# A two-layer attention/S5 backbone on one core: the last two SSM blocks' spans placed behind the second block's states, the end of the down product laid out anew, and its norms without ScalarE's roots

## Chip, core and metric

One core of a Trainium2 chip runs the whole program. The metric is the device time of one execution in microseconds (us). The kernel before takes 1716.74 us (median of 3 runs, 1716.3 to 1719.77).

## What is computed

Two layers over 512 latent tokens and 256 context tokens of width 1024. Layer 0 mixes tokens by attention, layer 1 by a bidirectional S5 state-space layer; each is followed by a gated ConvFFN, and every sub-layer stands between two RMS norms with a shift, a scale and a gate. Cut to what the change touches (layer 0's ConvFFN, then layer 1's mixer):

```
h  = modulate(rms_norm(x, g_pre_ffn), shift, scale)
a  = conv3(h @ w_up) + conv_b                       # 2 x 2816 columns
x  = x + gate * rms_norm((silu(a_gate) * a_val) @ w_down, g_post_ffn)
h  = modulate(rms_norm(x, g_pre_mix), shift, scale) # input of the S5 layer
for d in (forward, reverse):                        # 64 groups of 16 channels, 64 complex states each
    hc = scan(lambda, B @ h_context)                # the context's final state is the latents' first
    hl = scan(lambda, B @ h_latent, start=hc_final)
    y += Re(C @ hl)
g  = gelu(y + d_skip * h)
o  = (g @ w_glu_a) * sigmoid(g @ w_glu_b)
```

All of it is float32.

## The kernel before

A float32 product runs as three TensorE (PE) matmuls over operands split into a high and a low part (`mm3`, L145 to L147). A weight tile of 128x1024 is loaded by SyncE (SP) into a `wraw` slot, its high part is written by ScalarE (ACT, L108) and its low part by VectorE (DVE, L109), or by GpSimd (POOL) where the plan calls the weight "pool". The result is a `whl` tile. The loads, the splits and the products are pipelined over a few slots each.

`run()` goes through the stages qkv, attention, wo (the attention's output product), ffn0 (layer 0's ConvFFN), ssm, glu and ffn1. The text speaks of these places:

- **ffn0, up product** (about 490 to 845 us). PE multiplies w_up; between the products it prepares the tables of the S5 layer. These tables (`QT`, `Ks`) are written to DRAM (`Qd`) by SP, two DMAs for each QT and four for each Ks, in the same queue as the weight loads.
- **ffn0, down product, two passes** (`ffn_down`, `dn` tiles). The first pass takes three token tiles, the second the last three latent ones (tiles 3, 4, 5). The activation's split `hs` (ACT L927, DVE L928) rotates over `nhs` slots. The last four weights of a pass (`ends=4`) are held, so that one tile can be finished after the other. In the second pass the context half of the S5 scan (`ssm_contexts`) runs beside the product; it reads matrices `Pt` (SP, L1391).
- **end of a pass** (`done`, `begin`, `end`). For each finished tile: gate and sum of squares (ACT L726, DVE L727), a root (`rsqrt`), the residual (DVE L732, then a store to `x2`), the next norm's sum of squares and root, the scale (POOL L1022) and the shift (DVE L1023). The result `po` goes through a DMA into `xc`. The gate, shift and scale rows are loaded by `rows_of` (L996).
- **rsqrt** (L157 to L170). With `self.bits` it is eight small DVE instructions (a bit trick and three Newton steps), without it five on DVE and a square root on ACT, which needs another activation table.
- **ssm**. `ssm_turn` copies `xc` to `xq` (L1405) and turns it on PE (`pu`, L1410). `ssm_inputs` multiplies by the `Pt` matrices (`pi`, L1435) into B. `ssm_spans` (L1460 to L1464) scans spans of eight positions in seven steps on DVE: spans[0] and spans[1] serve blocks 0 and 1 (256 elements a partition each), spans[2] blocks 2 and 3 together (512). `local(i)` carries over the span ends in seven serial steps of four small instructions (L1473 to L1476) for blocks 2i and 2i+1. `states(blk)` adds the carries to all positions (L1591, L1595, L1602), `outputs(blk)` multiplies by the `Qd` matrices on PE (`py`, L1620), `turned(blk)` turns the result (`pg`, L1640), splits it into `gT` (DVE L1646) and multiplies by a GLU weight.

The order of each engine's instructions is set when the program is built: a scheduler with a model of times places them, engine by engine. `tc.issue_after(x)` gives the instructions traced inside it an order behind x, but only those on x's own engine. `W.behind` uses it for weight splits. In `ssm` the loop over the blocks reads:

```
first(0); local(0)
for blk in range(4):
    if blk == 2:
        first(1); local(1)
    turned(blk, outputs(blk, states(blk)))
```

`first(1)` runs spans[2] to its end. Nothing before the change holds it behind `states`.

Of the kernel before, what the change touches and what calls it, by code (L numbers as in the profile page):

```python
# [9 lines left out]
FT = mybir.dt.float32  # L10
# [3 lines left out]
AF = mybir.ActivationFunctionType  # L14
OP = mybir.AluOpType
# [4 lines left out]
P = 128  # L20
# [111 lines left out]
class Kernel:  # L132
# [619 lines left out]
    def wo(self):  # L752
        tc, nc = self.tc, self.nc
        self.ps = ps = tc.alloc_tile_pool(name="psC", bufs=1, space=PSUM, reuse_waits="tile")
        self.kv.release()
        self.bits = False
        self.actc = self.pool("actB1", "right")
        self.actp = self.pool("actB0", "right")
        late = self.pool("late", "right")
        wk = self.pool("wkC", "right")  # L760
        self.xd = self.dram.tile([TOK, D], FT, name="xd0")
        self.act = [[p.tile([P, 2, n], FR, name=f"b{n}_{kk}") for kk in range(KD)]
                    for p, n in ((self.actp, LAT), (self.actc, CTX))]
        acts = ((self.act[0], CTX, TOK, 0), (self.act[1], 0, CTX, 0))
        gates = [self.row(wk, 0, 1, 0, lc, f"gate{lc}", 1) for lc in range(2)]
        xn = {}

        def each(t, acc):
            x = self.post(t, acc, gates, self.x_rows, wk, 2)
            nc.sync.dma_start(self.xd[t * P:(t + 1) * P, :], x)  # L770
            xn[t] = self.renorm(x, late)
            if t % 2 and t > NTC:
                turn(t - 1, range(KD // 2))

        def turn(t, kps):
            self.transpose_norm(ps, late, [xn[t], xn[t + 1]], self.cols[0, 1], int(t < NTC), acts, t * P, kps)

        def turn_last():

            for kp in range(KD // 2):  # L780
                turn(0, (kp,))
                yield
            late.release()

        self.turn_last = turn_last()
        for i, tiles in enumerate(WO):
            if i == 2:
                self.conv_cols(0, self.actc, late)
            acc = {t: ps.tile([P, D], FT, name="wo", tag="big", bufs=3) for t in tiles}
            for b in range(2):  # L790
                self.proj_block(tiles, self.OT, ps, (lambda t, _: each(t, acc[t])) if b else (lambda t, _: None),
                                out=lambda t: acc[t][:, b * 512:(b + 1) * 512], last=b == 1 and tiles is WO[-1])
        wk.release()
        self.oq.release()
        self.qo.release()
# [167 lines left out]
    def ffn0(self):  # L963
        tc, nc, v, ps = self.tc, self.nc, self.nc.vector, self.ps
        self.x2 = self.dram.tile([TOK, D], FT, name="xd1")
        self.bits = False
        src = lambda t: self.xd[t * P:(t + 1) * P, :]

        def firsts():
# [36 lines left out]
        begun, loaded = [], {}  # L1006

        def begin(t, acc, wk, rows):
            begun.append((t, self.post_start(t, acc, [r and r[0] for r in rows], src, wk, 3, 3 if rows[1] else 2,
                                             loaded.pop(t))))  # L1010
            if len(begun) > 1:
                end(wk, rows)

        def end(wk, rows):

            t, x = begun.pop(0)
            x, o = x()
            if t >= NTC:
                nc.sync.dma_start(self.x2[t * P:(t + 1) * P, :], x)
            _, sh, gs = rows[int(t < NTC)]  # L1020
            r = self.stats(x, wk.tile([P, D], BF, name="junk", tag="junk", bufs=1), "sx")
            nc.gpsimd.tensor_tensor(o, x, gs, op=OP.mult)  # L1022
            self.mark = v.scalar_tensor_tensor(o, o, r, sh, op0=OP.mult, op1=OP.add).ins  # L1023
            if t < NTC:
                nc.sync.dma_start(self.xnd[t * P:(t + 1) * P, :], o)
                return
            c, q = D // 2, nc.scalar if t == NT - 1 else nc.sync
            for a in range(2):
                p0 = NCL * a + t - NTC
                q.dma_start(xc[p0:p0 + NCL - NT + NTC + 1:NT - NTC], o[:, a * c:(a + 1) * c])  # L1030
# [22 lines left out]
        sb1 = self.pool("ssmB1", "right")  # L1053
        self.sb, self.xc = [sb0, sb1], xc
        su = self.su = self.pool("ssmu", "right")
        self.hsp = self.pool("hsc")
        self.W.fence = self.W.limit = self.glu0
        jobs = self.ssm_contexts()
# [3 lines left out]
        def before():  # L1062
            for _ in jobs:
                pass
            rest["wk"] = wk = self.pool("wkE1")
            rest["rows"] = [rows_of(wk, 0), None]
            load(wk, tiles)
            self.sx = self.pool("ssmx", "right")
            self.mats = self.ssm_ahead([(self.Pd, gp, 2) for gp in range(0, G // 2, 2)],
                                       ((self.wp, "raw", 5), (self.sx, "Pt", 3)))  # L1070
            next(self.mats)

        tiles = range(NTC + 1, NT)

        def done(t, acc):
            done_of(rest["wk"], rest["rows"], tiles)(t, acc)

        self.ffn_down(tiles, ((0, P, LAT),), 4, done, jobs=(24, 4, 15, jobs), ends=4, before=before)
        rest["wk"].release()
        self.hsp.release()  # L1080
        self.hps[0].release()


# [247 lines left out]
    def plan_glu(self):  # L1331
        I, nc = self.I, self.nc
        for b in range(4):
            for c in range(4):
                srcs = [I[n][0].rearrange("(h c p) n -> c p h n", h=2, p=P)[c, :, :, b * 256:(b + 1) * 256]
                        for n in ("w_glu_a", "w_glu_b")]
                self.W.add("pool" if b == 0 else "split", *[
                    lambda t, j=j, src=src: nc.sync.dma_start(
                        t.rearrange("p (k h n) -> p k h n", k=2, h=2)[:, :, j, :], src)
                    for j, src in enumerate(srcs)])  # L1340
# [56 lines left out]
    def ssm_turn(self, src, xq, o, engines, tiles=1):  # L1397


        nc, n = self.nc, len(engines)  # L1400
        src = src.rearrange("p s (g c) -> p g s c", c=GC)
        k = src.shape[1] // n
        for i, e in enumerate(engines):
            x, y = xq[:, k * i:k * i + k], src[:, k * i:k * i + k]
            nc.scalar.activation(x, y, AF.Copy) if e is nc.scalar else e.tensor_copy(x, y)  # L1405
        xf = xq.rearrange("p g s c -> p g (s c)")
        for h in range(src.shape[1] // 4):
            p = self.bank([P, 4, P], "pu")
            for j in range(4):
                nc.tensor.transpose(p[:, j], xf[:, 4 * h + j], self.ident)  # L1410
            x, y = p.rearrange("p j (a c) -> p j a c", c=o.shape[-1]), o[:, 4 * h:4 * h + 4]
            if tiles > 1:
                x, y = x.rearrange("p j a (c t) -> p j a t c", t=tiles), y.rearrange("p j a (t c) -> p j a t c", t=tiles)
            if h % 2:
                nc.vector.tensor_copy(y, x)
            else:
                nc.scalar.activation(y, x, AF.Copy)
            yield
# [30 lines left out]
    def ssm_spans(self, pool, B, blk):  # L1449

        nc, v = self.nc, self.nc.vector
        nb, ns = B.shape[1], B.shape[2] // 8
        lr, li = (x[:, 0, blk:blk + nb].rearrange("p b r d g -> p b r (d g)") for x in self.lam)
        L = B.rearrange("p b (s k) r d g -> p b s k r (d g)", k=8)
        shape = [P, nb, ns, 2, 16]
        lr, li = (x[:, :, None].to_broadcast(shape) for x in (lr, li))
        for k in range(1, 8):
            t1 = pool.tile(shape, FT, name="t1", tag="t1", bufs=2)
            t2 = pool.tile(shape, FT, name="t2", tag="t2", bufs=2)
            v.tensor_tensor(t1, L[:, :, :, k - 1], lr, op=OP.mult)  # L1460
            for b in range(nb):
                v.tensor_tensor(t2[:, b], L[:, b, :, k - 1, ::-1], li[:, b], op=OP.mult)
            v.tensor_tensor(L[:, :, :, k], L[:, :, :, k], t1, op=OP.add)
            self.mark = v.tensor_tensor(L[:, :, :, k], L[:, :, :, k], t2, op=OP.add).ins  # L1464
            yield
# [62 lines left out]
    def ssm(self):  # L1528
# [18 lines left out]
        for gp in self.ssm_inputs(self.mats, lambda b: B[b // 2][:, b % 2, 1:], lambda g: u[:, g], NCL,  # L1547
                                  lambda gp: gp < 16):
            for b in range(min((gp + 2) // 8, 2)):
# [4 lines left out]
        W.ensure(self.glu0 + 4)  # L1554
        qs = self.ssm_ahead([(self.Qd, gp, 1) for gp in range(G // 2)],
                            ((sp, "Qt", 8),))
        next(qs)
        sq = self.pool("ssmq")
        NL = NCL // 8

# [18 lines left out]
        def states(blk):  # L1579
# [19 lines left out]
            S = sq.tile([P, NCL, 2, 8], FT, name="S", tag="S", bufs=2)  # L1599
            for d in range(2):  # L1600
                y = Bb[:, 0:NCL, :, d]
                self.mark = v.tensor_tensor(S[:, ::-1] if d else y, y, z[:, :, :, d], op=OP.add).ins  # L1602
            return S

        def outputs(blk, S):
# [52 lines left out]
        local(0)  # L1658
        for blk in range(4):
            if blk == 2:  # L1660
                first(1)
                local(1)
            turned(blk, outputs(blk, states(blk)))
        sq.release()
        st.release()
# [159 lines left out]
```

## Time and profile before

| | us |
|---|---|
| median of 3 runs | 1716.74 |
| the profiled execution | 1719.02 |
| its span, first to last instruction | 1717.2 |
| PE busy | 1553.6 (90%) |
| DVE busy | 1062.9 (62%) |
| ACT busy | 698.8 (41%) |
| POOL busy | 91.7 (5%) |

The profile is one execution; its mean granted TensorE clock is 0.951 of full speed. An engine's busy time says little by itself: what counts is where PE stands still, and what ends its waits. In 40 slices of the span, PE is near full from slice 5 to slice 23, falls to 1 to 6 tenths from 1050 to 1200 us, and is full again after. That hole, between the end of the second down pass and the first GLU products, is where most of the change works.

### The profile page before, as it was taken

What the parts mean: (1) busy time and instruction counts of PE and PEld (TensorE: products, weight loads), DVE (VectorE), ACT (ScalarE), POOL (GpSimd) and SP (SyncE); (2) the same over time, 40 slices, a digit from 0 to 9 for tenths busy, and PEclk for the clock granted to TensorE, in tenths of its full rate; (3) what the DMA queues carried; (4) which work ended last, traced back from release to release, by engine and by line L of the source; (5) the groups of instructions that cost most, each with busy time, mean ns of one, the idle gap of its engine ahead of it and who ended that gap; (6) DMA issues with size and microseconds to landing.
All of it is one profiled execution on the core that took longest, in us unless ns stands there. A gap on an engine that the chain in (4) does not pass through costs nothing.

```text
span 1717.2 us, 25140 instructions
## 1 busy us (share of the span) xinstructions
PE 1553.6 (90%) x9652; PEld 1249.8 (73%) x9652; DVE 1062.9 (62%) x2143; ACT 698.8 (41%) x1396; POOL 91.7 (5%) x96
## 2 busy tenths in 40 slices
PE   5999789999999999999999995416999999999997
PEld 2775568888888887777888784404778887788886
DVE  4653687669777677677545656598135754545334
ACT  4465557756443333232444432311245543333322
POOL 0111230000000000000000101020011000000000
PEclk8999799999999999999999998657999999999999
DMA  9424550085455657776763784633435234432421
GB/s 304 138 74 142 170 185 25 39 287 198 151 154 155 194 156 226 153 210 157 223 238 123 243 264 156 211 109 93 154 113 160 82 98 123 126 112 95 163 74 49
DMA packets 222174, 262.96 MB, mean 153 GB/s; under 512 B 20975, under 2 KB 172439, under 8 KB 221415
## 3 DMA queue, kind: packets, MB, share of 16 engines
q1 hardware_dynamic: 221334, 260.76, 49.7%
q8 instruction: 76, 1.25, 0.3%
q10 hardware_dynamic: 336, 0.54, 0.1%
q14 instruction: 44, 0.35, 0.1%
q0 software_dynamic: 384, 0.07, 0.0%
HBM read 223.37 MB, written 35.85 MB: 151 GB/s over the span
## 4 chain that ended last, share of the span: by engine, by line
PE 74%; DVE 14%; DMA 6%; ACT 3%; issue 2%; SPq 2%; ACTq 0%; POOL 0%; DVEq 0%; POOLq 0%
PE up L145 11%; PE up L147 11%; PE up L146 11%; PE dn L146 4%; PE dn L145 4%; PE dn L147 4%; PE acc L145 2%; PE acc L147 2%; PE acc L146 2%; PE glu L147 2%; PE glu L145 2%; PE glu L146 2%; PE py L1620 2%; PE macc L287 1%; DMA wm<-in_w_mod 1%
## 5 line engine op out<-in xcount | busy, mean ns | idle before, releaser
L109 DVE TENSOR_TENSOR whl<-wraw,whl 128x1024 fp32r<-128x1024 f32 x202 | 245.9, 1221 | 211.4 <-ACT whl L108 207.9
L108 ACT ACTIVATE whl<-wraw 128x1024 fp32r<-128x1024 f32 x206 | 216.9, 1056 | 246.3 <-PE dn L147 127.4
L145 PE MATMUL up<-b,whl 128*128 128x256 f32 (+1 forms) x728 | 244.5, 338 | 2.6 <-ACT whl L108 1.3
L147 PE MATMUL up<-b,whl 128*128 128x256 f32 (+1 forms) x728 | 241.9, 334 | 0.5 <-DVE whl L109 0.5
L146 PE MATMUL up<-b,whl 128*128 128x256 f32 (+1 forms) x728 | 241.8, 334 | 0.0
L146 PE MATMUL dn<-whl,hs 128*128 128x512 f32 x440 | 173.5, 397 | 2.3 <-DVE whl L109 2.2
L147 PE MATMUL dn<-whl,hs 128*128 128x512 f32 x440 | 173.0, 395 | 0.0
L145 PE MATMUL dn<-whl,hs 128*128 128x512 f32 x440 | 171.4, 395 | 0.0
L145 PEld LDWEIGHTS up<-b,whl 128*128 128x128 f32 x728 | 136.8, 188 | 28.0 <-issue 10.3
L147 PEld LDWEIGHTS up<-b,whl 128*128 128x128 f32 x728 | 136.7, 189 | 16.5 <-issue 1.8
L146 PEld LDWEIGHTS up<-b,whl 128*128 128x128 f32 x728 | 137.3, 189 | 15.4 <-issue 1.6
L862 DVE SCALAR_TENSOR_TENSOR ga<-up,cw,ga 128x511 f32<-128x511 f32 (+1 forms) x132 | 86.8, 658 | 91.4 <-ACT ga L858 89.9
L146 PE MATMUL up<-c,whl 128*128 128x512 f32 (+1 forms) x384 | 142.6, 373 | 0.1
L147 PE MATMUL up<-c,whl 128*128 128x512 f32 (+1 forms) x384 | 141.9, 372 | 0.0
L145 PE MATMUL up<-c,whl 128*128 128x512 f32 (+1 forms) x384 | 140.8, 375 | 1.0 <-DVE c L338 1.0
L858 ACT ACTIVATE ga<-up,cw 128x512 f32<-128x512 f32 x66 | 46.5, 705 | 155.8 <-PE up L147 154.0
L862 DVE SCALAR_TENSOR_TENSOR h<-up,cw,h 128x511 f32<-128x511 f32 (+1 forms) x132 | 86.7, 657 | 33.6 <-ACT h L858 32.6
L146 PEld LDWEIGHTS dn<-whl,hs 128*128 128x128 f32 x440 | 83.8, 190 | 21.8 <-DVE whl L109 3.0
L147 PEld LDWEIGHTS dn<-whl,hs 128*128 128x128 f32 x440 | 83.7, 190 | 18.3
L145 PEld LDWEIGHTS dn<-whl,hs 128*128 128x128 f32 x440 | 83.1, 189 | 18.9 <-ACT hs L927 0.4
L145 PEld LDWEIGHTS up<-c,whl 128*128 128x128 f32 x384 | 71.3, 188 | 18.0 <-issue 4.5
L147 PEld LDWEIGHTS up<-c,whl 128*128 128x128 f32 x384 | 72.2, 188 | 13.4 <-issue 0.4
(352 smaller groups left out, 2876.4 us busy)
## 6 DMA issues: line engine op xcount, KB each, us to landing
wraw<-in_w_up SPq DMA_DIRECT2D x88, 512.0 KB
wraw<-in_w_mod SPq DMA_DIRECT2D x80, 512.0 KB
wraw<-in_w_down SPq DMA_DIRECT2D x66, 512.0 KB
Pt<-Pd SPq DMA_DIRECT2D x32, 512.0 KB
wraw<-in_w_o SPq DMA_DIRECT2D x24, 512.0 KB
Pt<-Qd SPq DMA_DIRECT2D x32, 384.0 KB
wm<-in_w_mod SPq DMA_DIRECT2D x16, 512.0 KB
Pd<-Pb SPq DMA_DIRECT2D x16, 512.0 KB
```

The source lines that it names most:

```text
L108: nc.scalar.activation(w[:, 0], r, AF.Copy)
L109: e.tensor_tensor(w[:, 1], r, w[:, 0], op=OP.subtract)
L145: nc.tensor.matmul(out, a[0], b[0], start=start, stop=False)
L146: nc.tensor.matmul(out, a[0], b[1], start=False, stop=False)
L147: nc.tensor.matmul(out, a[1], b[0], start=False, stop=stop)
L287: nc.tensor.matmul(acc[32 * q:32 * q + 32], self.cT[:, k, :], w[:, 256 * q:256 * q + 256], start=(k == 0), stop=(k == KD - 1))
L858: nc.scalar.activation(o, acc, AF.Identity, scale=c[:, 1:2], bias=c[:, 3:4])
L862: nc.vector.scalar_tensor_tensor(x, acc[:, a + s:b + s], c[:, tap:tap + 1], x, op0=OP.mult, op1=OP.add)
L1620: nc.tensor.matmul(y[hs, i], x, t[hs, 2 + 2 * ri + d], start=False, stop=ri + d == 2)
```

## The change

- `self.bits` is True from wo on: the norms of wo and ffn0 take eight DVE instructions and no ACT root. 24 roots and two activation table loads go from ACT.
- `po` has three slots in both down passes; it had two in the second.
- The scale of the next norm, `o = x*gs` (L1022), moves from POOL to DVE: six instructions of 128x1024.
- The rows of the second pass get a pool of their own and are loaded before the pass begins.
- `Pt` has two slots in the pool `sx`, not three. `hs` has three in the second pass, not four.
- The low parts of the first four GLU weights go from POOL to DVE.
- `t1` and `t2` of the spans have one slot each.
- `next(qs)`, the first loads of the `Qd` matrices, stands in `issue_after(self.turned_in)`, the last xq copy that was traced.
- `first(1)` and `local(1)` stand in `issue_after(self.stated)`, the last instruction of `states(1)`.

```
-        self.bits = False                                   # in wo
+        self.bits = True
...
-        self.bits = False                                   # in ffn0
...
-            begun.append((t, self.post_start(t, acc, [r and r[0] for r in rows], src, wk, 3, 3 if rows[1] else 2,
-                                             loaded.pop(t))))
+            begun.append((t, self.post_start(t, acc, [r and r[0] for r in rows], src, wk, 3, 3, loaded.pop(t))))
...
-            nc.gpsimd.tensor_tensor(o, x, gs, op=OP.mult)
+            v.tensor_tensor(o, x, gs, op=OP.mult)
...
+        rowp = self.pool("rowp")
+        rows = [rows_of(rowp, 0), None]
         self.hsp = self.pool("hsc")
...
-            rest["rows"] = [rows_of(wk, 0), None]
...
-                                       ((self.wp, "raw", 5), (self.sx, "Pt", 3)))
+                                       ((self.wp, "raw", 5), (self.sx, "Pt", 2)))
...
-        self.ffn_down(tiles, ((0, P, LAT),), 4, done, jobs=(24, 4, 15, jobs), ends=4, before=before)
+        self.ffn_down(tiles, ((0, P, LAT),), 3, done, jobs=(24, 4, 15, jobs), ends=4, before=before)
...
-                self.W.add("pool" if b == 0 else "split", *[
+                self.W.add("split", *[
...
-            nc.scalar.activation(x, y, AF.Copy) if e is nc.scalar else e.tensor_copy(x, y)
+            self.turned_in = (nc.scalar.activation(x, y, AF.Copy) if e is nc.scalar else e.tensor_copy(x, y)).ins
...
-            t1 = pool.tile(shape, FT, name="t1", tag="t1", bufs=2)
-            t2 = pool.tile(shape, FT, name="t2", tag="t2", bufs=2)
+            t1 = pool.tile(shape, FT, name="t1", tag="t1", bufs=1)
+            t2 = pool.tile(shape, FT, name="t2", tag="t2", bufs=1)
...
-        next(qs)
+        with tc.issue_after(self.turned_in):
+            next(qs)
...
-                self.mark = v.tensor_tensor(S[:, ::-1] if d else y, y, z[:, :, :, d], op=OP.add).ins
+                self.stated = v.tensor_tensor(S[:, ::-1] if d else y, y, z[:, :, :, d], op=OP.add).ins
...
             if blk == 2:
-                first(1)
-                local(1)
+                with tc.issue_after(self.stated):
+                    first(1)
+                    local(1)
```

The scheduler builds the whole program anew, so the rows of each engine move also where the diff shows nothing. Three places follow. Lines of the changed kernel from 1592 on are one higher than the same lines before (L1592 there is L1591 here).

DVE in the ssm stage, before: the end of the last of the seven steps of spans[2] (L1464 over blocks 2 and 3 together, 128x2x8x32), carries (`cw`), then the first rows of `states(0)`.

```order
L1464 TENSOR_TENSOR B<-B,t_11328 128x2x8x32
L1475 TENSOR_TENSOR cw<-cw,B 128x64 x2
L1476 TENSOR_TENSOR B<-cw 128x2x32 x2
L1591 TENSOR_TENSOR t_10963<-B,lam 128x1792
L1473 TENSOR_TENSOR cw<-B,lam 128x64
L1474 TENSOR_TENSOR cw<-B,lam 128x64
L1591 TENSOR_TENSOR z_10920<-cx,lam 128x8x224
L1591 TENSOR_TENSOR z_10921<-cx,lam 128x8x224
L1595 TENSOR_TENSOR B<-B,t_10963 128x8x224
```

DVE at the same place now: the last of the serial carries, `states(0)`, `states(1)`, and only then the first step of spans[2] (operands of 128x512).

```order
L1476 TENSOR_TENSOR B<-cw 128x2x32
L1592 TENSOR_TENSOR t_11015<-B,lam 128x1792
L1592 TENSOR_TENSOR z_10972<-cx,lam 128x8x224
L1592 TENSOR_TENSOR z_10973<-cx,lam 128x8x224
L1596 TENSOR_TENSOR B<-B,t_11015 128x8x224
L1603 TENSOR_TENSOR B<-B,z_10972 128x128x8
L1603 TENSOR_TENSOR S<-B,z_10972 128x64x16
L1592 TENSOR_TENSOR t_11181<-B,lam 128x1792
L1596 TENSOR_TENSOR B<-B,t_11181 128x8x224
L1603 TENSOR_TENSOR B<-B,z_10973 128x128x8
L1603 TENSOR_TENSOR S<-B,z_10973 128x64x16
L1460 TENSOR_TENSOR t_11337<-B,lam 128x512
```

All seven steps of spans[2] and the carries of `local(1)` moved from ahead of `states(0)` to behind `states(1)`.

PE at the end of the second down pass, before: the last weight (whl195) over tile 5 (dn_9240), the two other tiles being done earlier.

```order
L147 MATMUL dn_9240<-whl194_10221,hs_10227 128x512
L145 MATMUL dn_9240<-whl195_10224,hs_10230 128x512
L146 MATMUL dn_9240<-whl195_10224,hs_10230 128x512
L147 MATMUL dn_9240<-whl195_10224,hs_10230 128x512
L145 MATMUL dn_9240<-whl195_10224,hs_10230 128x512
```

PE there now (dn_9281, dn_9282 and dn_9283 are tiles 3, 4 and 5).

```order
L147 MATMUL dn_9283<-whl194_10258,hs_10264 128x512
L145 MATMUL dn_9281<-whl195_10261,hs_10267 128x512
L146 MATMUL dn_9281<-whl195_10261,hs_10267 128x512
L145 MATMUL dn_9282<-whl195_10261,hs_10267 128x512
L146 MATMUL dn_9282<-whl195_10261,hs_10267 128x512
L145 MATMUL dn_9283<-whl195_10261,hs_10267 128x512
L146 MATMUL dn_9283<-whl195_10261,hs_10267 128x512
L147 MATMUL dn_9281<-whl195_10261,hs_10267 128x512
```

The last weight comes last for all three tiles, so that all three are finished at the very end. Further up in the same product the context jobs (`pi`) stand two weights later than before.

SP in the up product of ffn0, before, around the load of weight 145 (wraw_8057; the load of weight 144 is wraw_8052).

```order
L809 DMA wraw_8052<-in_w_up 128x8x128
L1307 DMA Qd<-QT 64x4x128 x2
L280 DMA mbias<-in_b_mod 32x256 x4
L1250 DMA tab<-tabd_2131 128x512
L1250 DMA tab<-tabd_2132 128x512
L1250 DMA tab<-tabd_2132 64x512 x2
L1307 DMA Qd<-QT 64x4x128 x2
L809 DMA wraw_8057<-in_w_up 128x8x128
L1307 DMA Qd<-QT 64x4x128 x2
L1325 DMA Qd<-Ks 16x8x128 x4
```

SP there now (weight 144 is wraw_8076, weight 145 wraw_8081).

```order
L809 DMA wraw_8076<-in_w_up 128x8x128
L1307 DMA Qd<-QT 64x4x128 x4
L1325 DMA Qd<-Ks 16x8x128 x8
L1307 DMA Qd<-QT 64x4x128 x2
L1325 DMA Qd<-Ks 16x8x128 x4
L1307 DMA Qd<-QT 64x4x128 x3
L1325 DMA Qd<-Ks 16x8x128 x4
L1307 DMA Qd<-QT 64x4x128 x3
L1325 DMA Qd<-Ks 16x8x128 x4
L1307 DMA Qd<-QT 64x4x128 x2
L809 DMA wraw_8081<-in_w_up 128x8x128
```

Weight 145's load moved behind 34 table writes that follow weight 144's load; before, four table writes and eight small transfers lay between the two.

## Rows read from the trace of the kernel before

**Rows 1.** Busy time by stretch: from:to, us, then PE, PEld, DVE, ACT, POOL, clock, DMA.
```profile
1100.00:1150.00 50.00, 19.43 (x518) 17.43 (x518) 45.15 (x99) 17.36 (x30) 9.86 (x4) 0.74 0.54 180
1150.00:1200.00 50.00, 24.04 (x222) 18.16 (x223) 47.52 (x81) 6.33 (x11) 0.00 (x0) 0.68 0.26 79
```

**Rows 2.** Timeline of PE: start, us, instruction, in brackets idle time before it.
```profile
956.11 0.50 PE L146 MATMUL dn<-whl,hs 128*128 128x512 f32 x1 [2.16 <-DVE whl L109]
...
1024.44 3.32 PE L1435 MATMUL pi<-uc,Pt 128*64 128x32 f32 x64 [1.38 <-DMA Pt<-Pd]
...
1094.37 4.53 PE L1410 MATMUL pu<-ident,xq 128*128 128x128 f32 x20 [38.93 <-ACT xq L1405]
...
1169.35 1.12 PE L1620 MATMUL py<-Pt,B 64*64 64x128 f32 x8 [43.53 <-DVE B L1602]
...
1211.33 1.09 PE L1640 MATMUL pg<-ident,yg 128*128 128x128 f32 x8 [0.70 <-ACT yg L1622]
```

**Rows 3.** Timeline of DVE in the ssm stage.
```profile
1120.69 2.62 DVE L1460 TENSOR_TENSOR t<-B,lam 128x256 f32<-128x256 f32 x1
...
1130.83 0.42 DVE L1460 TENSOR_TENSOR t<-B,lam 128x256 f32<-128x256 f32 x1
...
1132.42 0.42 DVE L1460 TENSOR_TENSOR t<-B,lam 128x256 f32<-128x256 f32 x1
...
1150.20 0.68 DVE L1460 TENSOR_TENSOR t<-B,lam 128x512 f32<-128x512 f32 x1
...
1153.22 0.68 DVE L1460 TENSOR_TENSOR t<-B,lam 128x512 f32<-128x512 f32 x1
...
1162.14 3.95 DVE L1591 TENSOR_TENSOR z<-cx,lam 128x1792 f32<-128x1792 f32 x2
...
1177.41 0.22 DVE L1473 TENSOR_TENSOR cw<-B,lam 128x64 f32<-128x64 f32 x1
...
1178.20 0.23 DVE L1473 TENSOR_TENSOR cw<-B,lam 128x64 f32<-128x64 f32 x1
```

**Rows 4.** Timeline of POOL, 1050 to 1140 us.
```profile
1062.30 2.34 POOL L1022 TENSOR_TENSOR po<-px,rows 128x1024 f32<-128x1024 f32 x1 [109.53 <-DVE rsp L170]
...
1120.66 9.86 POOL L109 TENSOR_TENSOR whl<-wraw,whl 128x1024 fp32r<-128x1024 f32 x4 [39.15 <-ACT whl L108]
```

**Rows 5.** Page, costliest groups: low parts on DVE; count, busy us, mean ns.
```profile
L109 DVE TENSOR_TENSOR whl<-wraw,whl 128x1024 fp32r<-128x1024 f32 x202 | 245.9, 1221 | 211.4 <-ACT whl L108 207.9
```

**Rows 6.** Timeline of DVE, end of the second down pass.
```profile
1055.59 0.69 DVE L727 TENSOR_TENSOR po<-dn,rows 128x512 f32<-128x512 f32 x1 [3.88 <-DMA rows<-md]
...
1062.29 3.43 DVE L732 SCALAR_TENSOR_TENSOR px<-po,rsp,px 128x1024 f32<-128x1024 f32 x1
...
1074.27 0.69 DVE L727 TENSOR_TENSOR po<-dn,rows 128x512 f32<-128x512 f32 x1 [4.35 <-DMA xc<-po]
...
1093.69 1.43 DVE L1405 COPY xq<-xc 128x512 f32<-128x512 f32 x4 [8.63 <-DMA xc<-po]
```

**Rows 7.** Busy time by stretch, around two waits of PE; columns as in rows 1.
```profile
950.00:960.00 10.00, 7.84 (x27) 5.75 (x26) 8.61 (x17) 6.78 (x12) 2.41 (x1) 0.84 0.40 135
...
1020.00:1030.00 10.00, 8.62 (x111) 7.35 (x111) 8.14 (x29) 2.54 (x4) 0.00 (x0) 0.75 0.89 296
```

**Rows 8.** Timeline of SP's queue in the up product: start, us to issue.
```profile
789.35 0.55 SPq L809 DMA_DIRECT2D wraw<-in_w_up  x1
...
808.40 2.53 SPq L1325 DMA_DIRECT2D Qd<-Ks  x4
```

**Rows 9.** Timelines of ACT and PE in the up product: weights 128 and 145.
```profile
724.77 1.06 ACT L108 ACTIVATE whl<-wraw 128x1024 fp32r<-128x1024 f32 x1 [2.70 <-DMA wraw<-in_w_up]
...
793.38 1.06 ACT L108 ACTIVATE whl<-wraw 128x1024 fp32r<-128x1024 f32 x1 [0.21 <-DMA wraw<-in_w_up]
...
813.70 0.39 PE L145 MATMUL up<-b,whl 128*128 128x512 f32 x1
813.92 0.40 PE L146 MATMUL up<-b,whl 128*128 128x512 f32 x1
```

More of the change, by code (lines that the diff above doesn't have):

```diff
@@ L1075, in done @@
         def done(t, acc):
-            done_of(rest["wk"], rest["rows"], tiles)(t, acc)
-        self.ffn_down(tiles, ((0, P, LAT),), 4, done, jobs=(24, 4, 15, jobs), ends=4, before=before)
+            done_of(rest["wk"], rows, tiles)(t, acc)
+        self.ffn_down(tiles, ((0, P, LAT),), 3, done, jobs=(24, 4, 15, jobs), ends=4, before=before)
         rest["wk"].release()
         self.hsp.release()
+        rowp.release()
         self.hps[0].release()
```

## Prediction

> **What bounds the kernel now.** I read first where PE stands still, then, for each of these places, the chain that ends its wait. By stretches, PE is busy for 19.4 and 24.0 us of the two 50 us from 1100 to 1200, while DVE works 45.2 and 47.5 of them [rows 1]: there DVE sets the time. The timeline of PE names the two holes [rows 2]: 38.93 us up to 1094.37, from the last product of the down pass (E, at 1094.37 - 38.93 = 1055.44) to the turning of the S5 input (R), ended by a copy of `xq`; and 43.53 us up to 1169.35 (P), until DVE's first `states` write. Two smaller waits stand earlier, 2.16 us for a weight's low part and 1.38 us for a `Pt` load. Elsewhere PE is full, so a term counts only if it shortens one of these waits or makes a new one.
>
> **The wait for states(0).** Three pieces of DVE work change ahead of P.
> - spans[2] goes. Its steps start 3.02 us apart (1150.20, 1153.22 [rows 3]), each with one carry of `local(0)` threaded in: 7 x 3.02 = 21.1 us. The seven carries then run alone, 0.79 us each (1177.41 to 1178.20 [rows 3]): 5.5 us come back. Net 15.6 gained.
> - The low parts of four GLU weights leave POOL. While POOL makes them, 9.86 us from 1120.66 [rows 4], a DVE instruction that otherwise takes 0.42 us takes 2.62, and one span step lasts 10.14 us (1120.69 to 1130.83) instead of 1.59 (1130.83 to 1132.42) [rows 3]: 8.5 us lost. On DVE the four cost 4 x 1.22 = 4.9 [rows 5]. Net 3.6 gained.
>
> The Trainium skill, Perfetto Trace Analysis, § Optimizing Scalar/DVE Operations, says that where DVE is saturated, moving work to ScalarE or even GpSimd may make sense, and adds that the two share a read port, so that between these two it might not help. Its first half speaks against this change, and by it the four low parts would cost 4.9 us and give nothing; its second half is what rows 3 and 4 show, and I follow the rows.
>
> - `t1` and `t2` with one slot: all their writers and readers are on DVE, in order, so 0.
>
> That is 19.2 us. What is late next is block 2, since spans[2] must still be done. From P: the write of S(0) ends about 1.2 later, and states(1) takes 2 x 2.0 for L1591 and L1595 and 2 x 1.2 for L1602 (estimates from 3.95 for two L1591 [rows 3] and 1.22 for a low part of 128x1024 [rows 5]): P + 7.6. Seven steps without carries, 3.02 less four of about 0.13, take 17.5; four low parts of `gT` about 2; `local(1)` 5.5; states(2) up to B 3 x 1.98 + 2.0 + 1.2 = 9.1. Sum P + 41.7. PE turns block 1 at P + 41.98 (1211.33 [rows 2]) and wants block 2's state about 1 us later, so the wait there is 0 to 2 us; I take 1. **Gain 18**; bounds 8 (steps stay at 3.02 and block 3 waits too) and 20.
>
> **From E to R.** Before, DVE idles 3.88 us for the rows and begins the norms at 1055.59; the last ends at 1093.69 - 8.63 = 1085.06, 29.5 us later; then the DMA into `xc` and the copy take 9.3 us to R, 8.63 of it idle on DVE [rows 6].
> - Removed: the wait for a `po` slot, 4.35; and POOL's three scales, which slow DVE: one instruction takes 3.43 beside one of 2.34 [rows 4, 6], against 1.22 for a low part of the same size [rows 5], so 2.2 each, 6.6.
> - Added: three scales on DVE, 3 x 1.22 = 3.7, and three more small instructions in each of six norms, of which I let 1.5 us count in all (bounds 0 and 18 x 0.22 = 4, by the small operation of rows 3).
> - The norms are then 29.5 - 4.35 - 6.6 + 3.7 + 1.5 = 23.8 us.
> - The order puts the context jobs two weights later, and DVE's part of them with them. A weight's 18 products take 4.0 us at 0.22 each (813.70 to 813.92 between two products of the same width [rows 9]), so DVE, free at 1055.59 - 3.88 = E - 3.7 before, is free some 8 us later, at E + 4.5. The early rows therefore gain nothing by themselves. All three tiles end at E as well.
> - R = E + 4.5 + 23.8 + 9.3 = E + 37.6 instead of E + 38.9. With the tiles' chains overlapping, some of the waits for ACT inside the 29.5 go too, about 1. **Gain 2**; bounds -6 (nothing overlaps) and +8 (`xc` lands in half the time, the context jobs end earlier).
> - `issue_after(self.turned_in)` moves nothing: turned_in is the DVE copy, the loads inside are SP's, and SP's order still has the eight `Qd` loads right behind the last `xc` write. 0.
>
> **Earlier waits.** The idle 2.16 us at 956.11 come with a clock of 0.84 of full over 10 us, 1.6 us more; the idle 1.38 at 1024.44 with 0.75, 2.5 us more [rows 2, 7]. In the new order weight 178's low part stands two norms earlier on DVE, and the `Pt` loads of the contexts no longer stand behind weight loads on SP. **Gain 6** of 7.6; bounds 0 and 7.6.
>
> **The up product's SP queue.** Before, weight 145 is issued at 789.35, split from 793.38 (4.0 us to land) and first used at 813.70 (by the order, this product is its first) [rows 8, 9]: 18 us of margin after the split. Now 34 table writes stand between it and weight 144. Four writes take 2.53 us [rows 8], so 34 take 21.5. If the first of them goes at about 788 (before, two stand just ahead of 789.35), the load goes at 809.5, lands at 813.5, and after 1.06 on ACT and 1.22 on DVE is ready at 815.8: PE waits 2.1 us. Weight 128 is late already (ACT waits 2.70 for its load [rows 9]) and gets four more writes ahead of it, 2.5 us. **Loss 4**, since some of the writes come earlier too; bounds 0 and 20 (the writes wait for tables that DVE and PE make late).
>
> **The rest.** Three `hs` slots: the last `hs` waits for PE to leave weight 192, with twelve products of 0.22 us behind which it is made; norms of wo and ffn0 without ACT's root: small DVE work beside products that PE fills; ACT, at 41%, loses work that nobody waited for. If that cover fails, 24 norms x 3 x 0.22 = 16 us on DVE. `Pt` with two slots: the last load comes later, behind the `Qd` loads. **Loss 0.5**; bounds 0 and 6.
>
> **Sum.** 18 + 2 + 6 - 4 - 0.5 = 21.5. Against the profiled execution, 1719.02 (span 1717.2), that is 1697.5. The profiled execution lies 2.3 above the median of three, 1716.74, so the median becomes 1695.2: **1695 us**. A measurement can tell about 0.2%, 3.4 us, from no change.
>
> **Rivals.**
> - *Everything overlaps* (chance 0.15). No give-back at block 2, an early end of the contexts, the queue's writes early: 19.2 + 8 + 7.6 = 34.8, 1682. For it: each single wait has an end in the trace that something in the order removes. Against: five favourable ends at once.
> - *Block 2 becomes the wait* (0.12). DVE's chain from P to states(2) is as long as PE's way there (41.7 against 42). If steps stay at 3.02 us (7 x 0.5 = 3.6) and the `gT` parts stand badly (5), PE loses 8.6 more: 1704.
> - *The queue starves PE* (0.07). Slower than before. Weight loads stand behind writes of tables which PE itself makes and DVE evicts; a late eviction holds every later weight. If each of three loads (128, 145, 148) comes 12 us late, 36 are lost instead of 4: 1695 + 32 = 1727. It decides from a loss of some 29 on, which is 25 more than I forecast. For it: weight 128 waits already, and 145's margin of 18 us is less than the 21.5 of its writes. Against: the tables' jobs stand earlier between the products as well.
> - *POOL was not what slowed DVE* (0.08). If the long DVE instructions of rows 3 and 6 have another cause, a transfer for instance, the 8.5 and the 6.6 stay and ten instructions more stand on DVE: 1695 + 15 = 1710. Against: the slow ones begin within 0.03 us of POOL's.
>
> This is the case that the first half of the Trainium skill's sentence in Perfetto Trace Analysis, § Optimizing Scalar/DVE Operations, would give.
>
> - *The ordering of the Qd loads does act, or they land late enough* (0.05). Then `xc` lands up to 4 us sooner: 1691. That it does nothing is in my forecast.
>
> The forecast keeps 0.53.
>
> **Range and chances.** 1680 to 1710 takes in the first, second and fourth rival and the bounds of the up product's queue; it leaves out the third and the tails. Faster by over 0.2%: 0.88; within it 0.04; slower 0.08, nearly all of it the third rival.
>
> **What would show it.** Right: `states(0)` written some 55 us after R instead of 75 (P - R); no DVE instruction of 128x256 above 1 us in the spans; norms that follow one another without a wait for `xc`; PE full around 956 and 1024; a wait of PE or ACT for `wraw` of 2 to 5 us near 815. Wrong: a wait of over 5 us of `py` for block 2's S; E to R of 39 us or more; waits for weight loads over 10 us in the up product.

## The result, and the profile after

The changed kernel takes 1691.21 us, the median of four runs (1690.33 to 1694.05), where the kernel before took 1716.9 beside it (1716.3 to 1719.77): a ratio of 0.985, 95% interval 0.9833 to 0.9867. The profiled execution has a span of 1689.5 us against 1717.2, 27.7 less, and a mean clock of 0.961 against 0.951.

By the page of the changed kernel PE is busy for 1548.3 us (92%), DVE for 1071.1 (63%), ACT for 695.2 (41%) and POOL for 67.0 (4%).

Busy time by stretch, columns as in [rows 1]:

```profile
950.00:960.00 10.00, 10.00 (x46) 8.29 (x45) 10.00 (x26) 5.24 (x8) 0.00 (x0) 1.00 0.55 165
1020.00:1030.00 10.00, 10.00 (x127) 8.44 (x127) 9.73 (x28) 4.95 (x8) 0.00 (x0) 1.00 0.89 310
...
720.00:740.00 20.00, 15.12 (x89) 11.92 (x86) 10.08 (x16) 4.70 (x8) 0.00 (x0) 0.83 0.90 204
```

The first two answer to [rows 7]: both waits are gone and the clock is at full. The last is a new loss, in the up product; the kernel before has 16.86 us of PE and a clock of 0.91 there.

Timeline of PE, the places of [rows 2]:

```profile
1086.03 4.30 PE L1410 MATMUL pu<-ident,xq 128*128 128x128 f32 x20 [33.74 <-ACT xq L1405]
...
1140.84 1.12 PE L1621 MATMUL py<-Pt,B 64*64 64x128 f32 x8 [25.02 <-DVE B L1603]
...
1184.96 0.49 PE L1621 MATMUL py<-Pt,B 64*64 64x128 f32 x4 [0.99 <-DVE B L1603]
```

With E, R and P as in the prediction: E is 1086.03 - 33.74 = 1052.29, R 1086.03, P 1140.84.

| | before | after | gained |
|---|---|---|---|
| start to E | 1055.44 | 1052.29 | 3.1 |
| E to R | 38.93 | 33.74 | 5.2 |
| R to P | 74.98 | 54.81 | 20.2 |
| P to the end of the span | 547.9 | 548.7 | -0.8 |

The 3.1 of the first row is a difference. Counted at the same number of products, PE stands 7.7 us further back as the first down pass begins, and still 7.1 some 90 us into it (948.8 us into the span instead of 941.7). From there it gains 10.2 by E, over the rest of that pass and the second one with the contexts. [Rows 2, 7] put a price on 7.6 of these 10.2: waits of 2.16 and 1.38, and 1.6 and 2.5 of slow clock beside them. The other 2.6 are not placed. Which of the edits took the two waits away was not tried.

Timeline of DVE, from the contexts' last instruction to the copy into `xq`, against [rows 6]:

```profile
1055.29 0.22 DVE L1476 TENSOR_TENSOR C<-cw 128x64 f32<-128x64 f32 x1
1055.43 0.68 DVE L727 TENSOR_TENSOR po<-dn,rows 128x512 f32<-128x512 f32 x1
...
1070.74 1.28 DVE L732 SCALAR_TENSOR_TENSOR px<-po,rsp,px 128x1024 f32<-128x1024 f32 x1
...
1075.99 1.28 DVE L1021 SCALAR_TENSOR_TENSOR po<-po,rsx,rows 128x1024 f32<-128x1024 f32 x1
1085.40 1.43 DVE L1405 COPY xq<-xc 128x512 f32<-128x512 f32 x4 [8.12 <-DMA xc<-po]
```

There is no wait for the rows, none for a `po` slot, and an L732 takes 1.28 us where one took 3.43. But the norms begin at E + 3.1 instead of E + 0.15, since the contexts end at E + 3.2.

Timeline of DVE in the ssm stage, against [rows 3]:

```profile
1121.57 0.42 DVE L1464 TENSOR_TENSOR B<-B,t 128x256 f32<-128x256 f32 x1
1121.91 4.62 DVE L109 TENSOR_TENSOR whl<-wraw,whl 128x1024 fp32r<-128x1024 f32 x4
...
1148.23 0.68 DVE L1460 TENSOR_TENSOR t<-B,lam 128x512 f32<-128x512 f32 x1
...
1151.22 0.69 DVE L1460 TENSOR_TENSOR t<-B,lam 128x512 f32<-128x512 f32 x1
...
1153.94 0.69 DVE L1460 TENSOR_TENSOR t<-B,lam 128x512 f32<-128x512 f32 x1
```

The four low parts stand on DVE for 4.62 us, no span step is stretched, and spans[2] begins behind `states(1)`. A step of it without carries takes 1153.94 - 1151.22 = 2.72 us.

SP's queue in the up product, against [rows 8]:

```profile
726.62 1.26 SPq L809 DMA_DIRECT2D wraw<-in_w_up  x2
...
789.20 3.66 SPq L1307 DMA_DIRECT2D Qd<-QT  x4
...
813.61 1.27 SPq L1307 DMA_DIRECT2D Qd<-QT  x2
814.98 0.55 SPq L809 DMA_DIRECT2D wraw<-in_w_up  x1
```

The 34 writes take from 789.20 to 814.9, 25.7 us. PE, though, does not wait for weight 145: the products ahead of it are some 7 us later by then. It waits for weight 128, issued at 726.62 (720.29 before). PE there:

```profile
731.89 0.79 PE L145 MATMUL up<-b,whl 128*128 128x512 f32 x1 [4.84 <-ACT whl L108]
```

Before, PE's waits at this place were 1.30, 1.32 and 0.52 us.

### The profile page after: what moved, and what is told of

It reads as the page before. It is cut to its first block, busy times and chain, and to the rows that moved or that the text cites. A ratio compares the mean times of both kernels' runs of the same rounds, so it can differ in the third digit from the quotient of the medians.

```text
span 1689.5 us, 25153 instructions
## 1 busy us (share of the span) xinstructions
PE 1548.3 (92%) x9652; PEld 1245.0 (74%) x9652; DVE 1071.1 (63%) x2225; ACT 695.2 (41%) x1370; POOL 67.0 (4%) x86
## 4 chain that ended last, share of the span: by engine, by line
PE 80%; DVE 10%; DMA 4%; ACT 2%; SPq 2%; issue 1%; ACTq 0%; POOL 0%; DVEq 0%
PE up L145 12%; PE up L147 11%; PE up L146 11%; PE dn L145 6%; PE dn L146 6%; PE dn L147 6%; PE acc L145 2%; PE acc L147 2%; PE acc L146 2%; PE glu L147 2%; PE glu L145 2%; PE glu L146 2%; PE macc L287 2%; PE py L1621 1%; DMA wm<-in_w_mod 1%; PE wo L145 1%
## 5 line engine op out<-in xcount | busy, mean ns | idle before, releaser
L109 DVE TENSOR_TENSOR whl<-wraw,whl 128x1024 fp32r<-128x1024 f32 x206 | 250.8, 1222 | 175.5 <-ACT whl L108 173.9
L147 PEld LDWEIGHTS up<-c,whl 128*128 128x128 f32 x384 | 72.3, 188 | 13.4 <-issue 0.4
```

The costliest lines, as they stand in the source:

```text
L109: e.tensor_tensor(w[:, 1], r, w[:, 0], op=OP.subtract)
L147: nc.tensor.matmul(out, a[1], b[0], start=False, stop=stop)
```

## The experiments

All ten kernels were timed against the kernel before on their own chip. The markers are from each kernel's timeline of PE. E lies between 1048.4 and 1052.3 in the changed kernel and in e1, e3 and e6, which leave the work ahead of E as it is, so the stretches behind E tell more than the totals where an effect is small.

| | us | ratio (95%) | E | E to R | R to P |
|---|---|---|---|---|---|
| changed kernel | 1691.21 | 0.985 (0.9833–0.9867) | 1052.3 | 33.7 | 54.8 |
| e1_nospan | 1706.72 | 0.9952 (0.9934–0.9969) | 1048.4 | 33.2 | 71.5 |
| e2_spanonly | 1699.08 | 0.9901 (0.9879–0.9923) | 1051.8 | 39.6 | 57.6 |
| e3_glupool | 1694.86 | 0.9875 (0.9854–0.9896) | 1051.2 | 33.5 | 59.7 |
| e4_scalepool | 1700.66 | 0.9908 (0.9884–0.9931) | 1058.9 | 32.6 | 54.4 |
| e5_bitslate | 1683.4 | 0.981 (0.9791–0.9829) | 1045.6 | 32.5 | 54.6 |
| e6_qdheld | 1688.03 | 0.9833 (0.9812–0.9855) | 1049.9 | 30.0 | 55.4 |
| e7_both | 1680.87 | 0.9803 (0.9773–0.9833) | 1043.6 | 28.8 | 57.1 |
| e8_po2 | 1698.94 | 0.9899 (0.988–0.9919) | 1054.2 | 40.9 | 55.7 |
| e9_rowslate | 1693.77 | 0.9871 (0.985–0.9892) | 1050.2 | 37.8 | 54.4 |
| e10_both_pool | 1683.14 | 0.9813 (0.9796–0.983) | 1044.2 | 31.4 | 58.1 |

**The span ordering taken out of the change, and put alone into the kernel before.**

```
-                with tc.issue_after(self.stated):
-                    first(1)
-                    local(1)
+                first(1)
+                local(1)
```

> The changed kernel with first(1) and local(1) taken out of issue_after(self.stated): spans[2] and local(1) may stand ahead of states(0) on DVE again. Theory (spans[2] on DVE is what PE waits for): R to P grows from 54.8 by 7 steps of 3.02 less seven serial carries of 0.79, 15.6, to about 70 us; block 2 no longer waits (0.99); the whole takes 1691 + 15 = 1706 us. Rival (most of the 20 us between R and P comes from the low parts leaving POOL): R to P grows by 4 to 8 us only, 1695 to 1699 us.

The second run is the kernel before with this edit alone, the other way round.

> The kernel before with this one edit alone: first(1) and local(1) in issue_after(self.stated). Theory: R to P falls from 75.0 by 15.6 to about 59.4, a wait of about 1 us appears at block 2, and the whole takes 1717 - 15 = 1702 us; the stretch where POOL makes the low parts still holds DVE instructions of 2.6 us. Rival (the edit only pays together with the others, since DVE becomes the bound at block 2): PE waits 5 us or more for block 2's state and the whole takes 1707 us or more.

Timeline of PE without the ordering, then with it alone:

```profile
1081.54 3.90 PE L1410 MATMUL pu<-ident,xq 128*128 128x128 f32 x20 [33.18 <-ACT xq L1405]
...
1153.08 1.12 PE L1621 MATMUL py<-Pt,B 64*64 64x128 f32 x8 [39.16 <-DVE B L1603]
```
```profile
1091.33 3.97 PE L1410 MATMUL pu<-ident,xq 128*128 128x128 f32 x20 [39.58 <-ACT xq L1405]
...
1148.91 1.12 PE L1620 MATMUL py<-Pt,B 64*64 64x128 f32 x8 [27.09 <-DVE B L1602]
...
1193.02 0.49 PE L1620 MATMUL py<-Pt,B 64*64 64x128 f32 x4 [0.95 <-DVE B L1602]
```

R to P grows by 16.7 us without it and shrinks by 17.4 with it alone, and block 2 gives back a wait of 0.95. The ordering is the largest single part, some 16 to 17 us.

**The GLU weights' low parts back on POOL.**

```
-                self.W.add("split", *[
+                self.W.add("pool" if b == 0 else "split", *[
```

> The changed kernel with the low parts of the first four GLU weights on POOL again. Theory (POOL slows DVE): DVE instructions of 0.42 us take about 2.6 while POOL works; R to P is 8.5 - 4.9 = 3.6 us longer, 58.4 instead of 54.8, and the whole takes 1695 us. Rival (the long instructions had another cause, so POOL is free help): 4.6 us of low parts leave DVE, R to P 50.2, the whole 1687 us.

Timelines of POOL and of DVE beside it:

```profile
1111.88 9.82 POOL L109 TENSOR_TENSOR whl<-wraw,whl 128x1024 fp32r<-128x1024 f32 x4 [259.57 <-ACT whl L108]
```
```profile
1112.02 2.50 DVE L1460 TENSOR_TENSOR t<-B,lam 128x256 f32<-128x256 f32 x1
1114.45 2.58 DVE L1462 TENSOR_TENSOR t<-B,lam 128x256 f32<-128x256 f32 x1
```

R to P is 4.9 us longer; the total's interval overlaps the changed kernel's, so the rows decide. The four DVE instructions beside POOL's take about 2.5 us where the same ones take 0.42 without it, and nowhere else in the spans are they slow: this is POOL's doing. The Trainium skill, Perfetto Trace Analysis, § Optimizing Scalar/DVE Operations, says that work moved between these two may not help since they share a read port; these rows agree.

**The six scales back on POOL.**

```
-            v.tensor_tensor(o, x, gs, op=OP.mult)
+            nc.gpsimd.tensor_tensor(o, x, gs, op=OP.mult)
```

> The changed kernel with the scale of the next norm (six instructions) on POOL again. Theory: in the last norms DVE instructions beside POOL's take 3.3 to 3.5 us; E to R grows from 33.7 by 3 x (2.2 - 1.2) = 3 us to 36.7, and the whole takes 1694 us. Rival (taking 1.2 us off DVE's chain three times helps more than the contention costs): E to R 31, the whole 1688 us.

Timelines of PE, POOL (the last scale of the first pass) and DVE beside it:

```profile
987.50 1.97 PE L1410 MATMUL pu<-ident,xcc 128*128 128x128 f32 x8 [5.50 <-ACT xcc L1405]
...
1091.45 4.11 PE L1410 MATMUL pu<-ident,xq 128*128 128x128 f32 x20 [32.56 <-ACT xq L1405]
```
```profile
956.92 3.74 POOL L1020 TENSOR_TENSOR po<-px,rows 128x1024 f32<-128x1024 f32 x1 [4.01 <-DVE px L732]
```
```profile
957.16 1.22 DVE L109 TENSOR_TENSOR whl<-wraw,whl 128x1024 fp32r<-128x1024 f32 x1
958.30 2.38 DVE L161 SCALAR_TENSOR_TENSOR rsx<-rsx 128x1 f32<-128x1 f32 x1
```

The norms of the second pass in this run, first and last instruction on DVE:

```profile
1058.58 0.69 DVE L727 TENSOR_TENSOR po<-dn,rows 128x512 f32<-128x512 f32 x1
...
1081.90 1.29 DVE L1021 SCALAR_TENSOR_TENSOR po<-po,rsx,rows 128x1024 f32<-128x1024 f32 x1
```

Both expectations missed E to R, which is 1.2 us shorter. The norms themselves are longer, as the theory had it: 1083.19 - 1058.58 = 24.6 us instead of 21.8. What hides it is that the contexts end at E - 0.2 here and at E + 3.2 in the changed kernel, since E comes 6.6 us later. That loss ahead of E is what the total shows. A new wait of 5.50 us stands there, for the context's input, with a clock of 0.83 beside it from 980 to 1000 us (1.00 in the changed kernel). ACT's copy of that input (986.82) comes no later than in the changed kernel (988.24), so what differs is where the order puts PE's use of it. This run moves the scheduler's order along with the engine, so its total cannot price the three scales of the second pass; the last run does.

**The norms of wo and of the up product with ACT's roots again.** `bits` False in wo and ffn0, True from the first down pass on.

```
-        self.bits = True
+        self.bits = False
...
+        self.bits = True
```

> The changed kernel with self.bits False in wo and in the up product, and True only from the first down pass on, so that wo and the up product are ordered as in the kernel before. Theory (the 7.1 us that PE is late after the up product come with the new order there, the wait for weight 128 in it): PE's wait for weight 128 falls from 4.8 to about 3 us, E comes 5 to 7 us earlier than 1052.3, and the whole takes 1685 us. Rival (the late 7 us do not come from this order, but from the later parts of the change, which move work ahead): E stays within 2 us, 1690 to 1692 us.

PE at weight 128, then the same 20 us by stretch:

```profile
721.78 0.36 PE L145 MATMUL up<-b,whl 128*128 128x256 f32 x1 [1.30 <-DVE ga L862]
...
726.83 0.79 PE L145 MATMUL up<-b,whl 128*128 128x512 f32 x1 [2.06 <-ACT whl L108]
```
```profile
720.00:740.00 20.00, 16.59 (x84) 12.40 (x73) 9.15 (x14) 5.67 (x9) 0.00 (x0) 0.91 0.88 229
```

E comes 6.7 us earlier, and the waits near 956 and 1024 stay away. So the norms without ACT's root in wo and the up product, with the order that comes with them, cost the 7 us, and the down pass did not need them. All kernels bear this out: from one product (PE's 1600th, at 322 to 325 us) to another in the first down pass (the 5200th), PE takes 582.9 to 586.2 us in the seven that have these norms without the root, and 577.2 to 578.2 in the five that have ACT's. Whether DVE's added work or the changed order does it is not taken apart. At weight 128 the difference is 4.84 us of waiting against 1.30 + 2.06, and over the 20 us 1.5 us of busy PE.

**The Qd loads held back.** They are ordered behind a small transfer on SP that reads `xc`, in place of the ordering that moves nothing.

```
+        seen = self.dram.tile([2 * NCL, 2], FT, name="seen")
+        held = nc.sync.dma_start(seen, self.xc[:, 0, 0:2]).ins
...
-        with tc.issue_after(self.turned_in):
+        with tc.issue_after(held):
```

> The changed kernel with the eight Qd loads really behind the arrival of xc: a small SP transfer reads xc, and the loads are ordered behind it on SP, where before they stood in issue_after of a DVE instruction. Theory (the loads take the DMA engines from the last transfer into xc): DVE's wait for xc falls from 8.1 to about 4.5 us, E to R from 33.7 to about 30, the whole takes 1688 us; the loads still land well before P. Rival (the transfer into xc is slow by itself, or the loads now come late for py): E to R within 1 us, 1691 us or more.

SP's queue in the changed kernel:

```profile
1073.25 1.18 SPq L1028 DMA_DIRECT2D xc<-po  x2
1074.53 8.92 SPq L1391 DMA_DIRECT2D Pt<-Qd  x8
```

SP's queue and DVE with the loads held back:

```profile
1070.83 1.19 SPq L1028 DMA_DIRECT2D xc<-po  x2
1079.14 0.33 SPq L1537 DMA_DIRECT2D seen<-xc  x1
1079.52 6.02 SPq L1391 DMA_DIRECT2D Pt<-Qd  x8
```
```profile
1079.15 1.43 DVE L1405 COPY xq<-xc 128x512 f32<-128x512 f32 x4 [4.30 <-DMA xc<-po]
```

The last transfer into `xc`, tile 5's, is in another queue: ACT issues it. Its issue, and what each DMA queue moves around it (packets, MB, share of the 16 DMA engines), from 1077 to 1086 us in the changed kernel; the 0.52 MB of q10 are ACT's two transfers of 256 KB:

```profile
1077.31 1.29 ACTq L1028 DMA_DIRECT2D xc<-po  x2
...
q1 hardware_dynamic: 741, 2.02, 74.8%
q10 hardware_dynamic: 288, 0.52, 21.2%
```

and from 1074 to 1080 us with the loads held back:

```profile
1074.89 1.27 ACTq L1028 DMA_DIRECT2D xc<-po  x2
...
q10 hardware_dynamic: 288, 0.52, 32.8%
q1 hardware_dynamic: 57, 0.03, 2.6%
```

The wait for `xc` falls from 8.12 to 4.30 us and E to R by 3.8. The eight loads, of which SP issues the first 2.8 us ahead of ACT's transfer and seven behind its start, took that time from the transfer that PE's restart hangs on: its 288 packets take from 1079.70 to 1084.68 beside theirs, and from 1076.17 to 1078.44 without.

**Both together.** The edits of the two runs before this.

> The edits of the two runs before together. Theory: they work at different places and add, 1691 - 6 - 3.5 = 1681 to 1682 us. Rival: what E gains is lost again behind it, 1686 us or more.

```profile
1072.39 4.53 PE L1411 MATMUL pu<-ident,xq 128*128 128x128 f32 x20 [28.78 <-ACT xq L1406]
```

This is PE's timeline. The ratio of 0.9803 (0.9773 to 0.9833) is the lowest of all; 0.9803 / 0.985 is 0.995, some 8 us below the changed kernel, and the two intervals only touch. E comes 8.7 us earlier and E to R is 5.0 shorter. R to P gives back 2.3, of which 0.9 are PE's waits for `Pt` (2.98 and 0.78 instead of 1.47 and 1.36); the rest is not placed.

**Two `po` slots in the second pass again.**

```
-            begun.append((t, self.post_start(t, acc, [r and r[0] for r in rows], src, wk, 3, 3, loaded.pop(t))))
+            begun.append((t, self.post_start(t, acc, [r and r[0] for r in rows], src, wk, 3, 3 if rows[1] else 2, loaded.pop(t))))
```

> The changed kernel with two po slots in the second down pass, as before the change. Theory (the third slot takes away a wait of 4.35 us): tile 5's first gate waits about 4 us for the transfer of tile 3's po, E to R grows from 33.7 to about 37.5, the whole takes 1695 us. Rival (DVE is full with the other tiles' norms, so the slot is free by then): E to R grows by less than 1.5 us, 1692 us.

Timelines of DVE and of PE:

```profile
1074.55 0.69 DVE L727 TENSOR_TENSOR po<-dn,rows 128x512 f32<-128x512 f32 x1 [4.33 <-DMA xc<-po]
```
```profile
1095.02 4.53 PE L1410 MATMUL pu<-ident,xq 128*128 128x128 f32 x20 [40.87 <-ACT xq L1405]
```

The wait of [rows 6] is back at its old length (4.33, 4.35), but E to R is 7.1 us longer, not 4. The last tile's norm chain begins only behind that wait, at E + 20.4 instead of E + 11.6. It is shorter than with three slots, where it runs between the other tiles' steps (10.7 us instead of 13.4), but the norms as a whole end 6.1 later. The other 1.0 is a longer wait for `xc` (9.13).

**The second pass's rows loaded in the old place.**

```
-        rowp = self.pool("rowp")
-        rows = [rows_of(rowp, 0), None]
...
+            rest["rows"] = [rows_of(wk, 0), None]
```

> The changed kernel with the rows of the second pass loaded where they were before the change, from the pool of the last norms. Theory of the prediction (DVE's context work ends 3 us behind E, and the rows could land by then, so loading them early gains nothing by itself): E to R within 1 us of 33.7, 1691 us. Rival (the rows' room becomes free only as DVE's context work ends, so they land about 4 us after it wherever that end lies): DVE idles about 3.9 us for the rows again, E to R 37.6, the whole 1695 us.

Timeline of DVE, the contexts' last instruction and the norms' first:

```profile
1053.17 0.22 DVE L1474 TENSOR_TENSOR C<-cw 128x64 f32<-128x64 f32 x1
1057.13 0.69 DVE L727 TENSOR_TENSOR po<-dn,rows 128x512 f32<-128x512 f32 x1 [3.73 <-DMA rows<-md]
```

SP issues the rows at 1053.21, as the contexts end, and DVE waits 3.73 us for them: E to R is 4.1 longer. The total's interval overlaps the changed kernel's, so here the row decides, not the time.

**The three scales of the second pass alone on POOL, in the best kernel.**

```
-            v.tensor_tensor(o, x, gs, op=OP.mult)
+            (v if rows[1] else nc.gpsimd).tensor_tensor(o, x, gs, op=OP.mult)
```

> The best version so far (bits from the first down pass on, Qd loads held back; 1681 us, E to R 28.8) with the scale of the second pass's three norms alone on POOL. Theory (in the second pass POOL's relief and its slowing of DVE nearly cancel, minus 1.2 us of E to R when all six were on POOL, and the 5.5 us lost there lay in the first pass): E to R 27.6 and 1680 us, no wait for the context's input. Rival (the loss comes from any scale on POOL): 1684 us or more.

Timelines of POOL (the second of the three scales), of DVE beside it, and of PE:

```profile
1056.95 2.34 POOL L1021 TENSOR_TENSOR po<-px,rows 128x1024 f32<-128x1024 f32 x1 [1.67 <-DVE rsx L157]
```
```profile
1057.40 0.14 DVE L158 TENSOR_SCALAR rsx<-rsx 128x1 int32<-128x1 int32 x1
1057.58 1.73 DVE L160 SCALAR_TENSOR_TENSOR rsx<-rsx 128x1 f32<-128x1 f32 x1
```
```profile
1075.64 4.53 PE L1411 MATMUL pu<-ident,xq 128*128 128x128 f32 x20 [31.44 <-ACT xq L1406]
```

E to R grows by 2.7 us (28.8 to 31.4), against the theory's 27.6: the three scales are better on DVE, by 0.9 us each. The norms that follow the contexts grow by as much as in the run with all six scales (2.7 and 2.8). The total's interval overlaps that of the kernel it is compared with, so the rows decide.

## Why the prediction was right, and where its terms were off

The forecast was 1695, and the time is 1691.21; 21.5 us were to be gained, and 27.7 were by the spans, 25.7 by the medians. That the sum came so near is in part luck: the stretch from the up product to E and the one from E to R gave 4.2 and 3.2 us more than forecast, and the up product lost 3 more. Term by term:

- **The wait for states(0)**: 19.2 forecast for P - R, 20.2 measured; 1 us of wait for block 2 forecast, 0.99 measured, and 0.8 given back behind P in all. The two pieces hold when taken apart: spans[2] 15.6 forecast, 16.7 and 17.4 in the two runs; the low parts 3.6 forecast, 4.9 in the run. The steps without carries take 2.72 us, not 2.5, and a low part stands in `states(2)`: its B is written at P + 44.1 instead of P + 41.7. It costs PE no more, because PE turns block 1 at P + 41.7, as forecast, and has some 1.5 us of work behind that.
- **From E to R**: this is the term that was mis-sized, gain 2 forecast, 5.2 measured. The direction of each piece was right but for one. The contexts end at E + 3.2 (4.5 forecast), the norms take 1077.27 - 1055.43 = 21.8 us (23.8), the way through `xc` 8.76 (9.3). Apart: the third `po` slot is worth 7.1, where the prediction counted its 4.35 wait and 1 for overlap; the three scales 2.7 in each of the two runs that put them back on POOL, by the length of the norms, near the 6.6 - 3.7 = 2.9 that it counted. **"The early rows therefore gain nothing by themselves" was wrong**: loaded in the old place, they are issued only as the contexts end, so with contexts that end later the wait moves with them, and 4.1 us would have stood on top.
- **Earlier waits**: 6 of 7.6 forecast; both waits and the slow clock beside them went, and PE gained 10.2 over that stretch. They stay away with ACT's roots in wo and the up product too. That the place of weight 178's low part and of the `Pt` loads did it, as the prediction has it, fits the order but was not tried apart.
- **The up product's SP queue**: 4 forecast, 7 measured, for another reason than the one given. The 34 writes took 25.7 us (21.5), but weight 145 was not waited for. Weight 128, which got four more writes ahead of it, costs 4.84 - (1.30 + 1.32 + 0.52) = 1.7 us of waiting, and the clock of 0.83 instead of 0.91 over 20 us another 1.6, though in three of the six runs that keep this order it is 0.91 there. That is 3.3 of the 7; with ACT's roots in wo and the up product all of it is gone. Of the other 3 to 4, 1.3 are idle time of PE from 320 to 500 us (176.26 us busy instead of 177.56); where the rest lies stays open. So this loss belongs to the norms without ACT's root, which the prediction held for covered by products and put under *the rest*, 0.5 us for all of it with a bound of 6.
- **The Qd ordering** moves nothing, as forecast: SP issues the eight loads from 1074.53 on, right behind its own last `xc` write. But the last write into `xc` is not SP's, as the prediction took it to be: ACT issues it at 1077.31, and the loads run beside it. That a working ordering gains up to 4 us was a rival's price; the run gave 3.8.
- **POOL**: the rival that POOL was not what slowed DVE falls by the low parts' run, and for the scales by the length of the norms in the two runs with scales on POOL.

Not tried: four `hs` slots beside the early rows and the third `po` slot; three `Pt` slots, though PE's waits for `Pt` ahead of `states(0)` grew from 0.40 and 0.47 us to 1.47 and 1.36.

## What to carry to other kernels

Where one engine makes several blocks ahead of a waiting one, order the later blocks behind the first result that is wanted, and check that the next block's chain still ends in time: here 16 us came for a wait of 1. A buffer slot can be worth more than the wait that its lack shows, since it also lets the chains run between each other's steps: here 7.1 us for a wait of 4.3. A transfer that a restart hangs on can lose time to loads in another queue, so hold such loads back until it has landed (3.8 us). An edit that changes only which engine makes small norms can move a scheduler's whole order, so try it undone where no engine waited for it (wo and the up product, some 7 us).

## What the runs showed of the hardware

- POOL and DVE can hold each other up for a whole instruction, at every size met here. Beside POOL's 128x1024 operations a DVE instruction of 128x256 takes 2.50 us instead of 0.42, one of 128x1024 takes 3.43 instead of 1.28, and one of 128x1 takes up to 2.38 instead of 0.16 to 0.22. The small ones end with POOL's: in e4_scalepool POOL's last scale of the first pass ends at 956.92 + 3.74 = 960.66 and the L161 beside it at 958.30 + 2.38 = 960.68. POOL's is stretched in the same way: DVE's L109 ran until 957.16 + 1.22 = 958.38, and what is left of the 3.74 is 2.28, near the 2.34 of a scale that DVE does not hold up (e10_both_pool, 1056.95). Not every DVE instruction is held: beside that scale L158, with one tensor operand, takes its 0.14 us, and the L160 behind it, with two, takes 1.73, until 1059.31, as the scale ends at 1059.29. So a chain of small steps suffers more than its sizes say. The Trainium skill, SBUF — State Buffer, § SBUF: two separate sides, describes an exclusive lock that one of the two holds for its whole instruction while the other blocks; these ends agree with it.
- The transfer that PE's restart hangs on is slowed by loads in another queue: ACT issues it, and DVE waits 8.12 us for `xc` while SP's eight `Qd` loads run beside it, 4.30 with them held back. Issuing the eight took SP 8.92 us in the first case and 6.02 in the second.
